# One fp32 encoder layer on one core: norm rows copied to SBUF, a finale of its own for the last token block, high parts first in gate and up, another pace for the norms

## The chip, the cores and the metric

The kernel runs on 1 core of one Trainium2 chip. The core has five engines with one in-order instruction queue each: TensorE (PE in the profile: matmuls and transposes), VectorE (DVE), ScalarE (ACT), GpSimd (POOL), and SyncE (SP), which here only issues DMAs. Operands stand in SBUF (128 partitions), matmul results in PSUM. The metric is the device time of one execution in microseconds.

## What is computed

One inference step of one encoder layer over 1024 prompt frames and 32 sample frames, D_MODEL 1024, in fp32: three sub-layers with a norm before and a norm after each, and a shift, scale and gate (adaLN) from a conditioning vector.

```python
# x += 1/2 * gate1 * RMSNorm_post(SwiGLU_1(adaLN(RMSNorm_pre(x))))
# x +=       gate2 * RMSNorm_post(W_out [GN_a(mixerA) ; GN_b(mixerB)](adaLN(RMSNorm_pre(x))))
# x += 1/2 * gate3 * RMSNorm_post(SwiGLU_2(adaLN(RMSNorm_pre(x))))
def rmsnorm(x, g):
    y = x * lax.rsqrt(jnp.mean(x * x, axis=-1, keepdims=True) + EPS)
    return y * g
def adaln_in(x, g, shift, scale):
    return rmsnorm(x, g) * (1 + scale[:, None, :]) + shift[:, None, :]
def swiglu(h, w_gate, w_up, w_down):
    return (jax.nn.silu(h @ w_gate) * (h @ w_up)) @ w_down
```

D_FF is 2816, that is 22 blocks of 128. The two mixers are banded attentions (8 heads with a cache of 512 rows; 8 query heads over 2 key heads with sinks); the change does not touch them. The outputs are y for prompt and sample, and the new cache rows.

## The kernel before

**Tiling.** Features stand on the partitions, tokens on the free axis, in three token blocks: tb0 and tb1 of 384 tokens, tb2 of 288 (256 of the prompt, 32 of the sample). A product in fp32 is made of three matmuls (`mm3`): weight and input are each split into a high and a low part, and hi·hi, hi·lo and lo·hi are added in PSUM. A weight block is split when it is loaded: ACT copies the high part (L303), DVE subtracts it for the low one (L304).

**Stages.** ffn1, attention (72 tiles), W_out (`out_piece`), ffn2, finale. A feed-forward stage runs through pairs of 128-wide blocks of D_FF. For each block and token block it makes `gate` (24 matmuls) and `up` (24) in one PSUM bank each, then ACT makes Silu of gate (`sl`, L550), DVE multiplies it by up (L551), ACT and DVE split the product into `gg` (L553, L554), and four `dn` groups of 12 matmuls are added to `facc` on DVE (L579 in the first round, L581 after). `gate` and `up` take turns in a pool of three PSUM banks (`p1`), so that the fourth of them waits until the first has been read.

**Norms.** `sumsq` squares a block on ACT (L364, tile `sq`, four pairs of feature tiles), folds and adds the pairs on POOL and DVE (L368, L370), and adds them over the partitions in two PE groups of three matmuls, `pss` (L357). `rstd_cols` makes the inverse root in ten tiny DVE operations in a row (rv at L387 to L391, ry, rt at L334 to L338). After WAIT = 3 more steps of the generator, three small matmuls spread it as a row over all partitions, `pr` (L405). `pss` and `pr` take turns in one PSUM bank (`pc`), and the readers of a row read `pr` there: eight scalings `n` of a pre-norm (L420), followed by h_hi on ACT (L444) and h_lo on DVE and POOL (L446, L449), or eight scalings of a post-norm's block (L464), followed by adding the residual (L467). The group norm of the mixers alone copies its row to SBUF first (L1145).

**What sets the order.** Norms and residuals are generators in a list (`side`); the feed-forward loops call `step(n)` after each gate and each up, which advances the list's first generator by n yields: PACE = 2, FAST = 10 in a stage's first round, OUTSTEP = 6 after each piece of W_out. That gives the order in which the program is written. A scheduler of the framework then sets the order on each engine, and takes an instruction forward where its inputs and its tile are free. Tiles come from pools that rotate; `s_tile` is a pool of five SBUF buffers, from which `sl` and the group norm's row are taken.

**Finale.** y = x + gate · norm(ffn2): for each token block the gates are multiplied onto f (L1304 on ACT, L1306 on DVE, eight of them), PE transposes f to tokens first (`py`, L1313, four to a bank), and DVE scales it by the token's inverse root and adds x, which was transposed before (`px`, L1293, copied to `xp` by ACT, L1294), at L1315. One DMA for each tile of 128 tokens writes y.

Of the kernel before, what the change touches and what calls it, by code (L numbers as in the profile page):

```python
# [34 lines left out]

PACE = 2
FAST = 10
OUTSTEP = 6
# [25 lines left out]
MANUAL = False  # L64
WAIT = 3
PREP = 3
STAGES = ((0, 34), (37, 54))
# [7 lines left out]
def encoder_step(ctx: ExitStack, tc, x_prompt, x_sample, cache_a_k, cache_a_v, cache_b_k, cache_b_v,  # L75
# [248 lines left out]
    def mm3(ps, w, k, hi, lo, start, stop):  # L324
        te.matmul(ps, w[:, 0, k], hi, start=start, stop=False)  # L325
        te.matmul(ps, w[:, 0, k], lo, start=False, stop=False)  # L326
        te.matmul(ps, w[:, 1, k], hi, start=False, stop=stop)  # L327


    def rsqrt(v, n, m):  # L330
# [13 lines left out]

    def sumsq(src, kts, w, bank, ends, fold=True):


        n = len(kts) // 2
        pss = bank("pss")
        cols = token_cols(w)  # L350
        behind = []

        def add_up(sq, first, last):
            halves = (0,) if fold else (0, 1)
            for q in halves:
                for j, (c0, m) in enumerate(cols):
                    te.matmul(pss[:m, j:j + 1], sq[:, q, c0:c0 + m], ones, start=first and j == 0 and q == 0,  # L357
                              stop=last and q == halves[-1], skip_group_check=True)

        acc, first = None, True  # L360
        for c in range(n):
            k = kts[2 * c]
            sq = h_tile([128, 2, 384], "sq")
            ae.activation(sq[:, :, :w], src[:, k:k + 2, :w], AF.Square)  # L364
            if fold:
                e = SQE[c % len(SQE)]
# [11 lines left out]
        add_up(*behind.pop())  # L378
        return pss

# [14 lines left out]

    def mean_rstd(src, kts, w, scale, ends, bank=None):

        bank = bank or pc
        pss = yield from sumsq(src, kts, w, bank, ends)
        y = rstd_cols(pss, w, scale)  # L400
        for _ in range(waits[0]):
            yield
        pr = bank("pr")
        for j, (c0, m) in enumerate(token_cols(w)):
            te.matmul(pr[:, c0:c0 + m], y[:m, j:j + 1].to_broadcast([m, 128]), ident[:m, :m], start=True, stop=True)  # L405
        yield
        return pr

    def norm_h(x, tb, j, H, ahead=0):
        w = TB[tb][1]  # L410
        r = yield from mean_rstd(x, range(KT), w, 1.0 / D, JN)
        hi, lo = H[tb] = (u_tile(tb, "h_hi", F32R), u_tile(tb, "h_lo", F32R))
# [41 lines left out]
    def resid(f, tb, j):  # L454

        w = TB[tb][1]
        r = yield from mean_rstd(f, range(KT), w, 1.0 / D, JR)
        for c in range(KT // 2):
# [66 lines left out]
    def ffn(key, H, F, wg, wu, wd, per_group, key_out, after, beside=lambda ff, tb: None):  # L525
# [10 lines left out]
        for r, (gi, blocks) in enumerate(plan):  # L536
# [3 lines left out]
            def up(ff, tb):  # L540
# [19 lines left out]
            def down(tb, r=r, grp=grp, wds=wds, gs=gs):  # L560
# [9 lines left out]
                for mp in range(KT // 2):  # L570
# [11 lines left out]
                    if r == final[tb]:  # L582
                        next(own)
                    step(1)
                if r == final[tb]:
# [18 lines left out]
            if (gi, 2) == (gi, blocks[-1]):  # L604
                per_group(gi)
        late.pop()()

# [530 lines left out]
    def group_norm(tb, g):  # L1138
# [3 lines left out]
        hi, lo = OH[tb]  # L1142
        pr = yield from mean_rstd(O[tb], range(4 * g, 4 * g + 4), w, 2.0 / D, JG, p1)
        r = s_tile([128, 384], "rstd")
        ae.activation(r[:, :w], pr[:, :w], AF.Copy)  # L1145
        for c in range(2):
# [134 lines left out]

    def tokens_first(tb):

        xp = upool.tile([128, 3, KT, 128], F32, name="xp", tag="u", bufs=6)
        for i, (t, c0, n) in enumerate(token_tiles(tb)):
            xt = XP[tb, i] = xp[:, i]
            xr = rpool.tile([128, KT, 128], F32, name="raw", tag="r")
            dma.dma_start(xr[:, :, :n], xs_dram[2][tb][:, :, c0:c0 + n])
            yield
            for hf in range(2):  # L1290
# [4 lines left out]
                yield  # L1295

    def finale(tb):
        f, w = F3[tb], TB[tb][1]
        pss = yield from sumsq(f, range(KT), w, pc, JF, fold=FF)
        y = rstd_cols(pss, w, 1.0 / D)  # L1300
        for k in range(KT):
            for a, b, st in SEGS[tb]:
                if k % 2:
                    ae.activation(f[:, k, a:b], f[:, k, a:b], AF.Copy, scale=gcoef[:, 2, st, k:k + 1])  # L1304
                else:
                    ve.tensor_scalar(f[:, k, a:b], f[:, k, a:b], gcoef[:, 2, st, k:k + 1], None, op0=OP.mult)  # L1306
            yield
        for i, (t, c0, n) in enumerate(token_tiles(tb)):
            xt = XP[tb, i]
            for k0 in (0, 4):  # L1310
                pt = p1("py", (128, 4, 128))
                for k in range(4):
                    te.transpose(pt[:n, k, :], f[:, k0 + k, c0:c0 + n], ident)  # L1313
                o = xt[:n, k0:k0 + 4]
                ve.scalar_tensor_tensor(o, pt[:n], y[:n, i:i + 1], o, op0=OP.mult, op1=OP.add)  # L1315
                yield
            dst = y_sample[0] if t == SEQ else y_prompt[0, t:t + 128]
            dma.dma_start(dst.rearrange("t (k c) -> t k c", c=128), xt[:n])
            yield

    def beside(ff, tb):
        if ff == NF - 1 and tb < 2:
            for t in ((0, 1), (2,))[tb]:
                begin(("xp", t), tokens_first(t))

# [30 lines left out]
```

## Time and profile before

| what | value |
| --- | --- |
| median of 3 runs | 2212.97 us (2211.99 to 2215.68) |
| the profiled execution | 2217.6 us, of which its span 2215.8 us |
| mean granted TensorE clock in it | 0.984 |
| PE busy | 2161.6 us (98%), 14012 instructions |
| DVE busy | 1239.1 us (56%) |
| ACT busy | 697.8 us (31%) |
| POOL busy | 179.2 us (8%) |

The span runs from the first instruction to the last. PE is busy nearly all the time, and all other engines far less, so PE's pauses, the clock it was granted and the work it was given are what the time is made of.

### The profile page before, as it was taken

The page shows a single profiled execution, that of the slowest core. Times are in us where ns is not written, and L with a number is a line of the kernel's source. Part 1 is how long each engine was busy: PE and PEld are TensorE (multiplying, and loading weights), DVE is VectorE, ACT ScalarE, POOL GpSimd, SP SyncE. Part 2 cuts the span into 40 slices and gives each one's busy share as a digit, 9 for nine tenths or more (in the row PEclk, how much of TensorE's full clock was granted, in tenths as well). Part 3 has the DMA queues.
Part 4 walks back from the last instruction along what each step waited for, and adds up shares of the span by engine and source line. Part 5 has one row for each costly group of instructions (what it writes and reads, how often), then busy time and mean ns, then how long its engine had stood idle before and what let it go on. Part 6 is the DMA issues. An engine that isn't in the chain of part 4 may idle for free.

```text
span 2215.8 us, 33976 instructions
## 1 busy us (share of the span) xinstructions
PE 2161.6 (98%) x14012; PEld 2068.6 (93%) x14012; DVE 1239.1 (56%) x2425; ACT 697.8 (31%) x1450; POOL 179.2 (8%) x281
## 2 busy tenths in 40 slices
PE   6999999999999999899999899999999999999998
PEld 4999999999999999799787589999999999999998
DVE  5788667874333497677444865785333333333336
ACT  4411111111121253576444663542111111111133
POOL 1100000000000023001110313220000000000000
PEclk8999999999999999899999899999999999999999
DMA  9253334434122352111112121424211111111122
GB/s 323 93 153 118 111 96 124 143 101 129 39 66 69 101 184 93 38 39 30 50 30 62 46 77 67 134 86 120 66 58 39 57 39 39 58 38 58 39 69 79
DMA packets 200623, 186.03 MB, mean 84 GB/s; under 512 B 7597, under 2 KB 169813, under 8 KB 199317
## 3 DMA queue, kind: packets, MB, share of 16 engines
q1 hardware_dynamic: 200468, 183.87, 27.1%
q8 instruction: 110, 1.80, 0.3%
q14 instruction: 45, 0.36, 0.1%
HBM read 164.12 MB, written 22.86 MB: 84 GB/s over the span
## 4 chain that ended last, share of the span: by engine, by line
PE 90%; DVE 4%; DMA 3%; ACT 1%; issue 1%; POOL 0%; SPq 0%; ACTq 0%; DVEq 0%; POOLq 0%
PE dn L325 7%; PE dn L326 7%; PE dn L327 7%; PE gate L327 7%; PE gate L326 7%; PE up L327 7%; PE up L326 7%; PE gate L325 7%; PE up L325 7%; PE po L713 3%; PE S L752 2%; PE pq L325 2%; PE pq L327 2%; PE pq L326 2%; DMA raw<-in_w_gate_dram 1%; PE pp L776 1%
## 5 line engine op out<-in xcount | busy, mean ns | idle before, releaser
L326 PE MATMUL gate<-h_lo,w 128*128 128x384 f32 (+1 forms) x1056 | 340.2, 322 | 4.0 <-DVE h_lo L446 4.0
L325 PE MATMUL dn<-gg,w 128*128 128x384 f32 (+1 forms) x1056 | 341.4, 325 | 1.1 <-DVE facc L581 1.0
L581 DVE TENSOR_TENSOR facc<-dn,facc 128x768 f32<-128x768 f32 (+1 forms) x240 | 212.9, 889 | 230.2 <-PE dn L327 229.9
L326 PE MATMUL dn<-gg,w 128*128 128x384 f32 (+1 forms) x1056 | 340.6, 323 | 0.6 <-DVE gg L554 0.6
L325 PE MATMUL gate<-h_hi,w 128*128 128x384 f32 (+1 forms) x1056 | 341.0, 323 | 0.0
L327 PE MATMUL gate<-h_hi,w 128*128 128x384 f32 (+1 forms) x1056 | 340.4, 322 | 0.0
L325 PE MATMUL up<-h_hi,w 128*128 128x384 f32 (+1 forms) x1056 | 340.2, 322 | 0.0
L326 PE MATMUL up<-h_lo,w 128*128 128x384 f32 (+1 forms) x1056 | 340.0, 322 | 0.0
L327 PE MATMUL dn<-gg,w 128*128 128x384 f32 (+1 forms) x1056 | 340.0, 322 | 0.0
L327 PE MATMUL up<-h_hi,w 128*128 128x384 f32 (+1 forms) x1056 | 339.9, 322 | 0.0
L304 DVE TENSOR_TENSOR w<-raw,w 128x1024 fp32r<-128x1024 f32 x187 | 231.5, 1246 | 150.5 <-ACT w L303 150.3
L303 ACT ACTIVATE w<-raw 128x1024 fp32r<-128x1024 f32 x187 | 195.7, 1056 | 266.1 <-PE dn L327 103.5
L550 ACT ACTIVATE sl<-gate 128x384 f32<-128x384 f32 (+1 forms) x132 | 60.9, 462 | 563.9 <-PE gate L327 560.9
L551 DVE TENSOR_TENSOR sl<-sl,up 128x384 f32<-128x384 f32 (+1 forms) x132 | 68.5, 519 | 292.1 <-PE up L327 286.1
L326 PEld LDWEIGHTS gate<-h_lo,w 128*128 128x128 f32 x1056 | 198.6, 188 | 4.6 <-DVE h_lo L446 4.6
L325 PEld LDWEIGHTS dn<-gg,w 128*128 128x128 f32 x1056 | 199.2, 189 | 1.6 <-DVE facc L581 1.2
L326 PEld LDWEIGHTS dn<-gg,w 128*128 128x128 f32 x1056 | 199.2, 189 | 1.0 <-DVE gg L554 0.9
L327 PEld LDWEIGHTS dn<-gg,w 128*128 128x128 f32 x1056 | 199.1, 189 | 0.0
L325 PEld LDWEIGHTS gate<-h_hi,w 128*128 128x128 f32 x1056 | 198.7, 188 | 0.1
L327 PEld LDWEIGHTS gate<-h_hi,w 128*128 128x128 f32 x1056 | 198.7, 188 | 0.0
L327 PEld LDWEIGHTS up<-h_hi,w 128*128 128x128 f32 x1056 | 198.7, 188 | 0.0
L325 PEld LDWEIGHTS up<-h_hi,w 128*128 128x128 f32 x1056 | 198.5, 188 | 0.0
(224 smaller groups left out, 3367.4 us busy)
## 6 DMA issues: line engine op xcount, KB each, us to landing
raw<-in_w_mod_dram SPq DMA_DIRECT2D x56, 512.0 KB, 4.0
raw<-in_w_gate_dram SPq DMA_DIRECT2D x54, 512.0 KB, 4.0
raw<-in_w_up_dram SPq DMA_DIRECT2D x54, 512.0 KB, 4.7
raw<-in_w_down_dram SPq DMA_DIRECT2D x54, 512.0 KB, 4.5
raw<-in_w_in_dram SPq DMA_DIRECT2D x18, 512.0 KB, 4.3
wm<-in_w_mod_dram SPq DMA_DIRECT2D x8, 1024.0 KB, 7.4
raw<-in_w_out_dram SPq DMA_DIRECT2D x13, 512.0 KB, 4.5
xr<-xs SPq DMA_DIRECT2D x16, 384.0 KB, 3.5
```

The costliest lines, as they stand in the source:

```text
L303: ae.activation(w[:, 0], r, AF.Copy)
L304: ve.tensor_sub(w[:, 1], r, w[:, 0])
L325: te.matmul(ps, w[:, 0, k], hi, start=start, stop=False)
L326: te.matmul(ps, w[:, 0, k], lo, start=False, stop=False)
L327: te.matmul(ps, w[:, 1, k], hi, start=False, stop=stop)
L550: ae.activation(sl[:, :w], ps[0][:, :w], AF.Silu)
L551: ve.tensor_tensor(sl[:, :w], sl[:, :w], ps[1][:, :w], op=OP.mult)
L581: ve.tensor_tensor(o, ps[:, :, :w], o, op=OP.add)
L713: te.matmul(po[64 * h:64 * h + 64, :n], vsl(j, h, kn), PT(h, j, kn), start=j == 0, stop=j == nt - 1)
L752: te.matmul(S[:, c:ce], self.T[:, h, :], KQ[:, 0, 128 * k0 + c:128 * k0 + ce], start=True, stop=True)
L776: te.transpose(pp[:, j - j0, :], P[:, 128 * j:128 * j + 128], ident)
```

## The change

1. `mm_all` takes the place of the loop over `mm3` in gate and up: for all eight feature tiles first hi·hi and lo·hi, which read h_hi alone, then the eight hi·lo, which read h_lo.
2. `mean_rstd` copies the row `pr` by ACT to an SBUF tile `rstd` of the `s_tile` pool (L423 in the changed kernel), for all norms but the very first, so that the bank `pc` is free after the copy.
3. `apart`: for tb2's norms (but the first), both its residuals, one group norm and the finale, the last pair of square tiles is not folded; PE adds its two halves itself, in three `pss` groups instead of two (three instead of one in the group norm).
4. `OUTWAIT = 4` in the loop over W_out's pieces: four steps instead of three between sums and row.
5. `step(BEHIND)` with BEHIND = 5 instead of PACE in rounds that run over tb2 alone.
6. The finale: POOL makes 16 diagonal matrices of the gates (`dg`), and PE multiplies f with them, which turns and scales f at once, in place of a transpose (and of the eight gate operations of each block). The finales of tb0 and tb1 are drained ahead of the last `dn` of tb2. tb2 has its own finale: x is turned behind the last `dn`, the four full half tiles wait in two `p2` banks, the sample's tile goes over ACT and POOL, and six half-tile DMAs write it.

```diff
+    def mm_all(ps, w, hi, lo):
+        for k in range(KT):
+            te.matmul(ps, w[:, 0, k], hi[:, k, :], start=k == 0, stop=False)
+            te.matmul(ps, w[:, 1, k], hi[:, k, :], start=False, stop=False)
+        for k in range(KT):
+            te.matmul(ps, w[:, 0, k], lo[:, k, :], start=False, stop=k == KT - 1)
...
-            halves = (0,) if fold else (0, 1)
+            halves = (0,) if fold and not (apart and last) else (0, 1)
...
-    def mean_rstd(src, kts, w, scale, ends, bank=None):
+    def mean_rstd(src, kts, w, scale, ends, bank=None, apart=False, copied=True):
         bank = bank or pc
-        pss = yield from sumsq(src, kts, w, bank, ends)
+        if apart:
+            ends = (len(kts) // 2 - 2, len(kts) // 2 - 1)
+        pss = yield from sumsq(src, kts, w, bank, ends, apart=apart)
         y = rstd_cols(pss, w, scale)
+        del pss
         for _ in range(waits[0]):
             yield
         pr = bank("pr")
...
+        if copied:
+            r = s_tile([128, 384], "rstd")
+            ae.activation(r[:, :w], pr[:, :w], AF.Copy)
+            pr = r
         yield
         return pr
...
                 for s in range(2):
-                    for k in range(KT):
-                        mm3(ps[s][:, :w], wgu[ff][s], k, hi[:, k, :], lo[:, k, :], k == 0, k == KT - 1)
-                    step(FAST if gi == 0 else PACE)
+                    mm_all(ps[s][:, :w], wgu[ff][s], hi, lo)
+                    step(FAST if gi == 0 else BEHIND if blocks == (2,) else PACE)
                 sl = s_tile([128, 384], "sl")
                 ae.activation(sl[:, :w], ps[0][:, :w], AF.Silu)
...
+        if key_out == "y":
+            finish()
         late.pop()()
...
+    waits[0] = OUTWAIT
     while outs:
         out_piece()
         step(OUTSTEP)
+    waits[0] = WAIT
...
+                ge.tensor_scalar(DG[st][:, k, :], ident, gcoef[:, 2, st, k:k + 1], None, op0=OP.mult)
...
+    def turned(pt, f, k, c0, n, t):
+        te.matmul(pt, f[:, k, c0:c0 + n], DG[1 if t == SEQ else 0][:, k, :], start=True, stop=True)
...
-        for k in range(KT):
-            for a, b, st in SEGS[tb]:
-                if k % 2:
-                    ae.activation(f[:, k, a:b], f[:, k, a:b], AF.Copy, scale=gcoef[:, 2, st, k:k + 1])
-                else:
-                    ve.tensor_scalar(f[:, k, a:b], f[:, k, a:b], gcoef[:, 2, st, k:k + 1], None, op0=OP.mult)
-            yield
+        if last:
+            yield from last_finale(f, y)
+            return
...
-                    te.transpose(pt[:n, k, :], f[:, k0 + k, c0:c0 + n], ident)
+                    turned(pt[:n, k, :], f, k0 + k, c0, n, t)
```

**Where instructions stand now.** In the rows below the number in a name grows in the order in which the program is written; a row stands for one or several instructions of its engine, in their order.

*The start of ffn2, PE.* Before, tb1's second norm has its sums (`pss_13745`) in the middle of the stage's fourth product, and its row `pr_13806` 16 matmuls later, among the `dn` groups:

```order
L327 MATMUL dn_14298<-gg_14143,w_13994 128x384
L325 MATMUL dn_14284<-gg_14280,w_13999 128x384
L325 MATMUL dn_14298<-gg_14280,w_13999 128x384
L405 MATMUL pr_13806<-ident_96,ry_13794 128x128 x3
L326 MATMUL dn_14284<-gg_14280,w_13999 128x384
```

In the changed kernel the same norm (`pss_13811`, `pr_13862`) and tb2's residual (`pss_14073`) stand in one piece behind the third product, gate of the second block:

```order
L335 MATMUL gate_14181<-h_hi_13566,w_14016 128x384
L337 MATMUL gate_14181<-h_lo_13567,w_14016 128x384 x8
L369 MATMUL pss_13811<-ones_98,sq_13804 128x1 x3
L369 MATMUL pss_13811<-ones_98,sq_13815 128x1 x3
L420 MATMUL pr_13862<-ident_96,ry_13824 128x128 x3
L369 MATMUL pss_14073<-ones_98,sq_14067 128x1 x2
L369 MATMUL pss_14073<-ones_98,sq_14067 32x1
L369 MATMUL pss_14073<-ones_98,sq_14071 128x1 x2
```

Behind the rest of `pss_14073` follow its row `pr_14099` and then the fourth product, `up_14182`: no matmul of the feed-forward stands any more between these two norms' sums and rows.

*The start of ffn2, ACT.* Before, the stage's first Silu (`sl_14140`, of the first product `gate_14002`), with the load of its table, stands behind the last weight split and ahead of the squares of tb1's second norm, though it was written behind them:

```order
L1177 ACTIVATE fo_13667<-wo_13946 128x288
L303 ACTIVATE w_14516<-raw_14514 128x1024
L550 ACT_TABLE_LOAD
L550 ACTIVATE sl_14140<-gate_14002 128x384
L364 ACTIVATE sq_13746<-fo_13251 128x768
```

Now the same Silu (`sl_14175`, of `gate_14034`) stands behind the copy of tb2's residual row, `rstd_14103`, which takes a tile of the same pool and is written ahead of it:

```order
L376 ACTIVATE sq_14067<-fo_13695 128x2x288
L376 ACTIVATE sq_14071<-fo_13695 128x2x288
L423 ACTIVATE rstd_14103<-pr_14099 128x288
L568 ACT_TABLE_LOAD
L568 ACTIVATE sl_14175<-gate_14034 128x384
L571 ACTIVATE gg_14178<-sl_14175 128x384
```

Ahead of these rows on ACT stand, all new ahead of the Silu, tb1's residual row, the squares and the row of tb1's norm and its h_hi.

*The end of ffn1, PE.* The norm of tb0 ahead of attention: before, 62 matmuls of gate, up and dn lay between its last sums (`pss_6661`) and its row `pr_6696`, which stands inside a gate:

```order
L325 MATMUL gate_7060<-h_hi_623,w_6904 128x288
L326 MATMUL gate_7060<-h_lo_624,w_6904 128x288
L327 MATMUL gate_7060<-h_hi_623,w_6904 128x288
L405 MATMUL pr_6696<-ident_96,ry_6684 128x128 x3
L325 MATMUL gate_7060<-h_hi_623,w_6904 128x288
```

Now the row follows its sums (`pss_6671`) at once, and an up follows the row:

```order
L328 MATMUL dn_6796<-gg_6566,w_6180 128x384
L329 MATMUL dn_6796<-gg_6566,w_6180 128x384
L369 MATMUL pss_6671<-ones_98,sq_6675 128x1 x3
L420 MATMUL pr_6696<-ident_96,ry_6684 128x128 x3
L334 MATMUL up_6815<-h_hi_627,w_6586 128x288
```

The residual of tb1 (`pss_6792`, `pr_6857`), and in the first round of ffn1 the norm of tb2 (`pss_594`, `pr_621`), stand in the same way.

*The end of ffn1, ACT.* Before, the Silus of these rounds stood among weight splits, with no norm's row between (`gate_6593` is the product whose bank the up behind next takes):

```order
L550 ACTIVATE sl_6557<-gate_6477 128x384
L303 ACTIVATE w_6585<-raw_6583 128x1024
L303 ACTIVATE w_6590<-raw_6588 128x1024
L553 ACTIVATE gg_6560<-sl_6557 128x384
L550 ACTIVATE sl_6653<-gate_6593 128x288
```

The same product is `gate_6599` now, its bank goes to `up_6815`, and its Silu stands right behind the copy of that norm's row:

```order
L305 ACTIVATE w_6934<-raw_6932 128x1024
L305 ACTIVATE w_6939<-raw_6937 128x1024
L423 ACTIVATE rstd_6700<-pr_6696 128x384
L568 ACTIVATE sl_6702<-gate_6599 128x288
L376 ACTIVATE sq_6754<-facc_887 128x768
```

On DVE the low parts of `w_6934` and `w_6939` stand between the sums and the inverse root of this norm; before, two such splits stood there too.

More of the change, by code (lines that the diff above doesn't have):

```diff
@@ L36 @@
 PACE = 2
+BEHIND = 5
 FAST = 10
@@ L65 @@
 WAIT = 3
+OUTWAIT = 4
 PREP = 3
@@ L410, in norm_h @@
         w = TB[tb][1]
-        r = yield from mean_rstd(x, range(KT), w, 1.0 / D, JN)
+        r = yield from mean_rstd(x, range(KT), w, 1.0 / D, JN, apart=tb == 2 and j > 0, copied=tb > 0 or j > 0)
         hi, lo = H[tb] = (u_tile(tb, "h_hi", F32R), u_tile(tb, "h_lo", F32R))
@@ L1142, in group_norm @@
         hi, lo = OH[tb]
[L1143 to L1145 removed]
+        r = yield from mean_rstd(O[tb], range(4 * g, 4 * g + 4), w, 2.0 / D, JG, p1, apart=(tb, g) == (2, 0))
         for c in range(2):
```

83 lines of the change are left out of this document (67 added, 16 removed).

## The prediction, made before the changed kernel was timed

> **What bounds the kernel now.** I read the page's busy times first, then the chain that ended last, the clock and busy time by stretch, and PE's waits.
>
> ```profile
> PE 2161.6 (98%) x14012; PEld 2068.6 (93%) x14012; DVE 1239.1 (56%) x2425; ACT 697.8 (31%) x1450; POOL 179.2 (8%) x281
> PE 90%; DVE 4%; DMA 3%; ACT 1%; issue 1%; POOL 0%; SPq 0%; ACTq 0%; DVEq 0%; POOLq 0%
> ```
>
> PE is busy for 2161.6 of 2215.8 us and makes 90% of the chain. So a change can take away PE's pauses (54 us in all), the slow clock behind them, and PE work; and whatever holds PE up anew costs its full length. The stretches that the change touches, as columns: window, its length, busy us of PE, PEld, DVE, ACT, POOL (instructions), granted clock, DMA share, GB/s.
>
> ```profile
> 60.00:80.00 20.00, 18.16 (x100) 17.76 (x99) 17.48 (x35) 11.73 (x20) 4.61 (x5) 0.91 0.56 172
> 760.00:780.00 20.00, 20.00 (x141) 20.00 (x140) 15.94 (x31) 6.67 (x10) 3.66 (x2) 1.00 0.49 143
> 780.00:800.00 20.00, 20.00 (x148) 19.92 (x146) 17.85 (x29) 10.38 (x14) 5.66 (x4) 1.00 0.66 211
> 880.00:900.00 20.00, 14.53 (x98) 13.45 (x97) 15.07 (x50) 11.46 (x32) 5.81 (x10) 0.74 0.14 59
> 1320.00:1340.00 20.00, 17.05 (x113) 15.01 (x112) 8.47 (x30) 8.21 (x16) 2.86 (x4) 0.86 0.36 105
> 1340.00:1360.00 20.00, 19.78 (x113) 19.27 (x113) 13.33 (x25) 9.18 (x15) 11.23 (x8) 0.97 0.00 1
> 1420.00:1440.00 20.00, 19.38 (x110) 19.20 (x109) 15.54 (x34) 6.78 (x12) 7.64 (x6) 0.91 0.27 105
> 1440.00:1460.00 20.00, 17.87 (x98) 17.49 (x97) 15.82 (x31) 7.65 (x13) 3.80 (x4) 0.91 0.23 60
> ```
>
> Read them in pairs of idle time and clock. 760 to 800, the end of ffn1 where tb0's and tb1's norms run, has no pause at all: nothing can be won there, only lost. 60 to 80 (first round of ffn1) has 1.84 us of pause and a clock of 0.91, which is 1.8 us of clock missing, or 3.6 us at half speed: **one pause of about 2 us also costs about 1.8 us of half clock**. 880 to 900 (tb2's norm ahead of attention), 1320 to 1360 (group norm of tb2) and 1420 to 1460 (start of ffn2) show the same. Whom PE waited for there:
>
> ```profile
> PE pr L405 <- DVE ry L338: 4.8, 2, 2.4
> PE gate L326 <- DVE h_lo L446: 4.0, 2, 2.1
> PE pk L1057 <- DVE n L420: 1.9, 1, 1.9
> ```
>
> **Prices.** One place of before shows what a row costs that follows its sums with no matmul between (tb2's norm; timeline: start, length, engine, what, idle before):
>
> ```profile
> 884.89 0.91 PE L357 MATMUL pss<-ones,sq 128*32 128x1 f32 x8
> 885.83 0.16 DVE L388 TENSOR_SCALAR rv<-pss 128x2 f32<-128x2 f32 x1 [1.19 <-PE pss L357]
> ...
> 887.93 0.16 DVE L338 SCALAR_TENSOR_TENSOR ry<-rt,ry 128x3 f32<-128x3 f32 x1
> 888.24 0.98 PE L405 MATMUL pr<-ident,ry 128*128 128x128 f32 x3 [2.44 <-DVE ry L338]
> ```
>
> The **row wait** is 2.44 us. The other durations, from the groups of 700 to 900 us and the timeline at the start of ffn2:
>
> ```profile
> L446 DVE SCALAR_TENSOR_TENSOR h_lo<-n,modT,h_hi 128x384 fp32r<-128x384 f32 x12 | 9.4, 838 | 0.0
> L467 DVE TENSOR_TENSOR facc<-facc,xr 128x768 f32<-128x768 f32 x4 | 4.4, 1132 | 0.0
> L550 ACT ACTIVATE sl<-gate 128x384 f32<-128x384 f32 x5 | 2.4, 488 | 17.1 <-PE gate L327 17.1
> ...
> 1415.56 0.34 PE L327 MATMUL gate<-h_hi,w 128*128 128x384 f32 x1
> 1415.74 0.83 PE L405 MATMUL pr<-ident,ry 128*128 128x128 f32 x6
> 1417.86 1.28 ACT L550 ACT_TABLE_LOAD   x1
> 1417.88 1.23 DVE L304 TENSOR_TENSOR w<-raw,w 128x1024 fp32r<-128x1024 f32 x1 [4.09 <-ACT w L303]
> 1419.02 4.28 DVE L464 SCALAR_TENSOR_TENSOR fo<-fo,gcoef,pr 128x384 f32<-128x384 f32 x8
> 1431.55 0.80 PE L357 MATMUL pss<-ones,sq 128*128 128x1 f32 x6 [0.62 <-DVE sq L370]
> ```
>
> A 384-wide matmul starts 0.18 us after the one before (1415.56 to 1415.74), so gate or up of 24 takes 4.2; the 288-wide ones 3.2 in proportion. A row's copy is not in the trace: another 128x384 read of PSUM by ACT, Silu, takes 0.49, and I take that (nothing if it were hidden, 0.6 at most). In the changed order a Silu stands right behind the copy of a row, and the next up needs that Silu's bank. So each such row has a **hold**: copy 0.49, Silu 0.49, two hand-overs, 1.1 us (1.0 for 288). A `pss` group is 0.7 (0.91 for eight records, of which a group has six).
>
> **The change, stage by stage.**
>
> *First round of ffn1.* High parts first and the copied rows remove the pause on h_lo and its half clock: −3.6. New: tb1's row is followed by the hold (1.1), tb2's sums come 0.6 late, its row follows at once (2.44), then another hold (1.0): 5.1, and half clock behind two of these pauses (2 × 1.8): +8.7. Net **+5.1** (+2 to +8).
>
> *End of ffn1, tb0 and tb1.* Nothing is removed. Along the four norms: (1) tb0's residual: 3.1 us of matmuls cover the row wait; hold 1.1; then `dn` waits for gg's low part, which DVE makes behind two scalings, two adds of 1.1 and a weight split, 1.8. (2) tb0's norm: row wait 2.44 and two weight splits of 1.23 inside the chain, 4.9; hold 1.0. (3) tb1's residual: its sums stand on DVE behind eight scalings (4.3), six h_lo (5.0 at 838 ns), Silu's products, a split and folds, about 13 us from the row, while PE has gate, up and four `dn`, 7.2, behind the hold: 4.7; then 0.4 of a split, 2.44 and a hold of 1.0; the next gate waits for a bank whose reader stands behind eight scalings, 1.0. (4) tb1's norm: 12 `dn` (1.6) lie between sums and row, but the chain of 2.44 has an addition to facc and two splits inside, 5.6: 4.0; hold 1.0. Together 23.3. PE bounds only some of the work between, so I put half clock behind three pauses, 5.4: **+28.7** (+13, bare row waits and holds, to +37).
>
> *tb2's norms ahead of attention.* BEHIND ends the other chains early; 5 to 6 us of other products now lie between tb2's sums and both rows, and the bank is free for `pk`. The stretch 880 to 900 loses 5.5 us of pause, and 0.26 × 20 = 5.2 us of missing clock, of which some 3.3 fall on work: −8.8; two more `pss` groups: +1.4. **−7.4** (−8.8 to −4).
>
> *Group norm of tb2.* 19 matmuls of W_out (0.18 each at 384, 3.4) cover the row wait of 2.44. Gone are 3.2 us of pause (2.95 and 0.22) and 3.4 of missing clock, less what falls on the pauses: −6.1, plus two groups 1.4: **−4.7** (−6 to −2). OUTWAIT moves rows only among W_out's matmuls, which keep PE busy: nothing; if that cover were gone, a row wait.
>
> *Start of ffn2.* Count from the end of tb1's residual row. PE has 21 matmuls of up and 24 of gate: 8.0 us, then only sums and rows until the Silu. DVE and ACT: copy 0.5; from the first scaling (1419.02) to the second sums (1431.55) before took 12.5, less 0.5 for one product that now comes later: sums at 12.5, row wait from 13.2, row done at 16.5. Copy 0.5, scalings 4.3, six h_lo 4.7 (between 0.7 and 0.84), folds 1.0: tb2's sums start at 27.0 and take 2.1, row wait, row: 32.4. Copy, table 1.28, Silu: the fourth product starts at 34.7. Of the 26.7 us since 8.0 PE works 5.0: 21.7 of pause. Behind it tb2's norm: row wait 2.44, hold 1.0, a bank 1.8. Half clock behind three pauses 5.4. Sum +32.3. Gone are 2.75 us of pause and 0.18 × 20 = 3.6 of half clock: **+26** (+14 to +34).
>
> *Finale.* Rows of the chain:
>
> ```profile
> 2189.73 0.44 PE py L1313 x4
> 2198.49 0.67 DVE facc L581
> 2206.39 0.18 DVE ry L334
> 2208.36 0.76 DVE xp L1315
> 2212.09 0.74 DVE xp L1315
> ```
>
> A transpose is 0.11; an fp32 product with a diagonal is not shown, but three such products of `pr` take 0.83, 0.28 each, and two records of transposes 0.22, which I take (0.11 to 0.28). The 48 of tb0 and tb1 come ahead of the last `dn`: 2.6 more for tb0, 5.3 for tb1, 2.6 less for tb2's turned x: last `dn` +5.3. Behind it 16.9 us remain before (2198.9 to 2215.8); now sums after about 5.3, root 2.3, four scalings 2.7, and 3.0 to the end as before: 13.3. **+1.7** (−3 to +5).
>
> Sum: 5.1 + 28.7 − 7.4 − 4.7 + 26 + 1.7 = 49.4. The profiled execution took 2217.6, so 2267; the median of the three runs is 4.6 lower: **2262**.
>
> **Rivals.**
>
> *Bare waits.* DVE and ACT are ahead more than I count, and only row waits (seven of 2.44, one of them half covered) and holds remain, without half clock: low ends, 2 + 13 − 8.8 − 6 + 14 + 0 = +14, **2227**. For it speaks the engine's share of 56%; against it, 760 to 800 shows DVE busy 16 to 18 of 20.
>
> *No clock loss.* If pauses of 1 to 3 us leave the clock alone, the 14.4 us of half clock fall out: **2248**. The row 60 to 80 speaks against it. [...]
>
> *Rows from SBUF are slow to read.* The group norm's scalings, which read a copied row, against those that read PSUM (1300 to 1400 us):
>
> ```profile
> L1150 DVE SCALAR_TENSOR_TENSOR z<-o,cst,rstd 128x384 f32<-128x384 f32 x4 | 3.4, 900 | 0.0
> L420 DVE SCALAR_TENSOR_TENSOR n<-fo,acoef,pr 128x384 f32<-128x384 f32 x8 | 4.3, 608 | 0.0
> ```
>
> 0.29 more for each of eight scalings in five chains that PE now waits for is +11.7: **2274**. [...]
>
> *The other side: not slower.* Removed are 3.6 + 8.8 + 6.1 + 6.3 = 24.8 us. If every new pause is bare and short, ffn2's Silu comes after tb1's row instead of tb2's in effect (sums ready when PE arrives), then seven row waits and eight holds are 24.5, less 4 that pieces of `dn` cover: −4, **2209**. It decides once the start of ffn2 pauses for less than about 8 us. The order of ACT, in which that Silu stands behind tb2's copied row, speaks against it.
>
> **How the numbers follow.** My forecast 45%, bare waits 19%, no clock loss 14%, slow rows 13%, not slower 9%. The range takes in the forecast's neighbours, half of the bare case and the slow rows: 2229 to 2284. A measurement tells about 0.2% (4.4 us) from no change. Faster 4%, same 5%, slower 91%.
>
> **What would show it.** Right: PE's waits list `pr` behind DVE's ry with some 15 to 20 us in seven or more pauses, up behind ACT's Silu with 10 or more; 740 to 800 no longer full; a pause of 15 us or more in pieces behind the third product of ffn2, and none at 880 to 900 and 1330. Wrong: PE still full over 740 to 800, or the first Silu of ffn2 starting within 10 us of its gate; then the Silus do not wait for the rows.

## The result, and the profile after

| | before | changed kernel |
|---|---|---|
| median, us (4 runs each) | 2213.64 | 2295.53 |
| lowest to highest, us | 2211.99 to 2215.68 | 2294.24 to 2295.83 |
| profiled execution, us (its span) | 2217.6 (2215.8) | 2294.24 (2292.4) |

The changed kernel is slower: the ratio is 1.0369, with a 95% interval of 1.0353 to 1.0386. That is 82 us, where 49 were forecast, and the time lies above the range.

The page of the changed kernel, busy times of the engines and the chain that ended last:

```profile
PE 2185.3 (95%) x14132; PEld 2095.1 (91%) x14132; DVE 1238.4 (54%) x2401; ACT 696.6 (30%) x1450; POOL 192.9 (8%) x297
PE 34%; DVE 1%; ACT 0%; issue 0%; POOLq 0%; POOL 0%; ACTq 0%; DVEq 0%
```

PE is busy 24 us longer, but the span grew by 76.6: PE's pauses went from 54 to 107 us. DVE's total is as before (1238.4 against 1239.1): the changed finale takes some 13 us off it (1225.9 in e7 below) and slower scalings put 14 back (1224.0 in e3, without them). What the pauses come from is shown by the experiments.

Busy time by stretch of the changed kernel; columns as in the prediction (window, length, busy us of PE, PEld, DVE, ACT and POOL, granted clock, DMA share, GB/s):

```profile
780.00:800.00 20.00, 15.22 (x99) 14.57 (x99) 18.29 (x20) 6.04 (x8) 8.32 (x5) 1.00 0.46 158
800.00:820.00 20.00, 12.62 (x71) 12.03 (x69) 17.34 (x31) 12.82 (x21) 6.16 (x5) 0.74 0.20 55
820.00:840.00 20.00, 13.28 (x69) 12.64 (x70) 15.63 (x29) 4.23 (x7) 6.28 (x4) 0.66 0.48 160
1460.00:1480.00 20.00, 10.68 (x55) 10.01 (x53) 13.94 (x27) 4.52 (x7) 7.84 (x6) 0.72 0.19 80
1480.00:1500.00 20.00, 5.20 (x24) 4.74 (x24) 13.54 (x32) 8.58 (x16) 5.20 (x5) 0.50 0.20 59
```

The end of ffn1, which was full, and the start of ffn2 now have long pauses, and the granted clock is low behind them, down to 0.50 where PE is busy for 5.2 of 20 us. Whom PE waited for, over the whole span (us in total, times, longest):

```profile
PE pr L420 <- DVE ry L348: 20.5, 7, 4.6
PE pss L369 <- POOL sq L382: 16.4, 4, 5.9
PE pss L369 <- DVE sq L382: 14.2, 2, 12.3
...
PE up L334 <- ACT sl L568: 8.6, 8, 2.3
PE gate L334 <- DVE sl L569: 3.2, 2, 1.7
```

Rows wait for the inverse root in seven places, sums wait for the squares, and up waits for the Silu eight times. Gate waits for what the Silu is multiplied into. Before, the first kind was 4.8 in two places, and no matmul waited for a Silu.

The table cuts the span at the same matmuls of both traces and gives what each stretch takes longer than before, in us. The first round of ffn1 and the start of ffn2 run from the first to about the 200th gate of their stage, the end of ffn1 from the 1441st gate to the first product of attention. The last columns are experiments told of below.

| stretch | forecast | changed | e1 | e2 | e3 | e4 | e11 |
|---|---|---|---|---|---|---|---|
| first round of ffn1 | +5.1 | +10.2 | +9.7 | +0.6 | −1.3 | +11.9 | +0.5 |
| end of ffn1 | +28.7 | +37.7 | +22.0 | −0.2 | +0.3 | +22.0 | −0.3 |
| tb2's norms ahead of attention | −7.4 | −7.9 | −2.1 | +12.4 | +4.9 | −1.0 | +1.6 |
| attention, to its last product | | −5.3 | −5.2 | −6.4 | −5.2 | −4.3 | −3.2 |
| W_out, group norm of tb2 | −4.7 | +4.7 | +0.5 | +3.8 | +4.6 | +4.0 | −0.8 |
| start of ffn2 | +26 | +33.1 | +30.8 | +0.7 | −3.9 | +32.5 | −4.1 |
| finale (to last dn, and behind it) | +1.7 | +4.8 | 0 | +4.4 | +4.6 | +4.1 | −0.6 |

Attention is shorter in every kernel, even where nothing near it was touched. In the profiled execution of before, the time from the first `S` product to the first product of W_out is 213.7 us at a mean granted clock of 0.95; it is 209.5 at 0.98 in the changed kernel and 209.1 at 0.98 in e7, which changes nothing there. So this row is in the main the clock of that one execution, which fits its lying above its median. How far two executions differ elsewhere shows in e3 and e6, which have the same lines in both feed-forward stages: their first rounds of ffn1 differ by 2.4 us and their starts of ffn2 by 2.5. A single step of that size says little.

### The profile page after: what moved, and what is told of

It reads as the page before. It is cut to its first block, busy times and chain, and to the rows that moved or that the text cites. A ratio compares the mean times of both kernels' runs of the same rounds, so it can differ in the third digit from the quotient of the medians.

```text
span 2292.4 us, 34227 instructions
## 1 busy us (share of the span) xinstructions
PE 2185.3 (95%) x14132; PEld 2095.1 (91%) x14132; DVE 1238.4 (54%) x2401; ACT 696.6 (30%) x1450; POOL 192.9 (8%) x297
## 5 line engine op out<-in xcount | busy, mean ns | idle before, releaser
L334 PE MATMUL gate<-h_hi,w 128*128 128x384 f32 (+1 forms) x1056 | 332.1, 323 | 4.4 <-DVE sl L569 3.2
L335 PE MATMUL gate<-h_hi,w 128*128 128x384 f32 (+1 forms) x1056 | 330.1, 322 | 0.0
L334 PEld LDWEIGHTS up<-h_hi,w 128*128 128x128 f32 x1056 | 204.4, 194 | 10.3 <-ACT sl L568 10.3
L335 PEld LDWEIGHTS up<-h_hi,w 128*128 128x128 f32 x1056 | 204.5, 194 | 0.0
L337 PE MATMUL gate<-h_lo,w 128*128 128x384 f32 (+1 forms) x1056 | 196.2, 322 | 0.6 <-DVE h_lo L465 0.6
L337 PE MATMUL up<-h_lo,w 128*128 128x384 f32 (+1 forms) x1056 | 193.0, 324 | 0.0
L337 PEld LDWEIGHTS up<-h_lo,w 128*128 128x128 f32 x1056 | 174.6, 191 | 0.0
```

Of the source, the lines that this page charges most:

```text
L334: te.matmul(ps, w[:, 0, k], hi[:, k, :], start=k == 0, stop=False)
L335: te.matmul(ps, w[:, 1, k], hi[:, k, :], start=False, stop=False)
L337: te.matmul(ps, w[:, 0, k], lo[:, k, :], start=False, stop=k == KT - 1)
```

## The experiments

Each kernel was measured beside the kernel before on the same chip, so its ratio counts more than its microseconds. Where an expectation names theories by letters: A is that the copied rows take tiles from the pool of the Silus (`s_tile`, five tiles, handed out in program order), so that a Silu, and PE behind it, stands behind a norm's row; C is that other parts of the change cost the time; H, that half clock does; G, that the chain of the group norm has a length of its own; S, that scalings which read a row from SBUF are slow beside POOL.

**e1: of the whole change, the copies alone.**

```diff
         pr = bank("pr")
...
+        if copied:
+            r = s_tile([128, 384], "rstd")
+            ae.activation(r[:, :w], pr[:, :w], AF.Copy)
+            pr = r
```

> The kernel before, with part 2 alone: every row but the first is copied into a tile of the pool from which Silu's tiles come. Theory A (the Silus stand behind the rows, because a pool hands out its tiles in the order in which the program asks for them, so PE has no free bank and waits for rows): nearly all of the loss is there, 2265 to 2292 us, with the steps of the first round of ffn1 (about +10) and of the start of ffn2 (about +33) as in the changed kernel, and a smaller one at the end of ffn1 (+15 to +35), since PACE 2 leaves matmuls between two of its norms' sums and rows. Rival C (the faster pace of rounds over tb2 alone, high parts first or the extra sums bring the pauses): 2210 to 2235 us.

Measured: 2273.56 us, ratio 1.0258 (1.0240 to 1.0275). These lines make 57 of the 82 us, at the three places where the changed kernel loses most. C falls as the main cause; what `BEHIND` adds is in e4.

**e2: the whole change, with the copies in tiles of another pool.**

```diff
-            r = s_tile([128, 384], "rstd")
+            r = h_tile([128, 384], "rstd")
```

> The changed kernel, rows copied all the same, but into tiles of the pool that holds the squares (one word changed). Theory A: the Silus stand ahead of the rows again, 2195 to 2215 us, and PE's waits list no up behind ACT's Silu. Rival B (the copy on ACT and the scalings that read SBUF are themselves the cost, about 0.5 us and 8 times 0.3 us at each of 20 rows on the path): still above 2270 us.

Measured: 2231.89 us, ratio 1.0070 (1.0055 to 1.0085). One word is worth 3.0%, some 66 us, with the same instructions, in another order. ACT's timeline at the start of ffn2 in this kernel (start, length, engine, line, what, idle before):

```profile
1426.06 1.28 ACT L568 ACT_TABLE_LOAD   x1
1428.87 0.49 ACT L568 ACTIVATE sl<-gate 128x384 f32<-128x384 f32 x1 [1.52 <-PE gate L337]
1430.11 0.49 ACT L423 ACTIVATE rstd<-pr 128x384 f32<-128x384 f32 x1 [0.75 <-PE pr L420]
```

The Silu waits only for its own gate, and stands ahead of the residual row; PE's waits list no up behind a Silu any more. In the changed kernel it stands behind that row and two more:

```profile
1458.54 0.49 ACT L423 ACTIVATE rstd<-pr 128x384 f32<-128x384 f32 x1 [4.01 <-PE pr L420]
...
1478.41 0.49 ACT L423 ACTIVATE rstd<-pr 128x384 f32<-128x384 f32 x1 [7.85 <-PE pr L420]
...
1498.26 0.41 ACT L423 ACTIVATE rstd<-pr 128x288 f32<-128x288 f32 x1 [9.82 <-PE pr L420]
1498.69 1.28 ACT L568 ACT_TABLE_LOAD   x1
1499.98 0.49 ACT L568 ACTIVATE sl<-gate 128x384 f32<-128x384 f32 x1
```

Its gate was done at 1457; the Silu runs at 1500. The mechanism is shown: with the pool, the order on ACT changes and the loss goes. But the level was expected at 2195 to 2215: tb2's norms ahead of attention lose 12.4 here where the changed kernel gains 7.9. In the changed kernel 5.5 us of other products lie between tb2's sums and its row; here PE waits 4.4 us for these sums, 2.4 for the row right behind them and 2.8 for an h_lo. `BEHIND` is in both kernels, so it brings that gain only together with the late end of ffn1, which costs more.

**e3: the whole change without the copies (only the group norm keeps its own).**

```diff
-        if copied:
+        if copied and bank is not pc:
```

> The changed kernel without part 2: rows stay in their bank, as before (the group norm keeps its copy). Theory A: 2195 to 2215 us, within 8 us of e2_rows_h; what separates the two is the price of the copies themselves. Rival B: 2195 to 2215 us too, but over 50 us under e2_rows_h. Rival C: above 2250 us.

Measured: 2226.71 us, ratio 1.0046 (1.0028 to 1.0063). The loss at the three places is gone. What remains are tb2's norms, the group norm and the finale, together some 14 us, and against them some 5 at the two places where high parts first was to gain. It was expected lower, as e2 was: the other parts of the change, taken together, do not pay either. Some 5 us lie between e2 and e3; so much do the copies cost when no Silu stands behind them.

**e4: the whole change without `BEHIND`.**

```diff
-                    step(FAST if gi == 0 else BEHIND if blocks == (2,) else PACE)
+                    step(FAST if gi == 0 else PACE)
```

> The changed kernel without part 5 (PACE 2 in the rounds over tb2 alone). Theory A: only the end of ffn1 changes, where two norms now have 5 us of matmuls between sums and row: its step falls from +38 to about +20, 2275 to 2283 us in all, while the first round of ffn1 and the start of ffn2 keep their +10 and +33. Rival C: the end of ffn1 loses its whole step, about 2258 us.

Measured: 2285.45 us, ratio 1.0310 (1.0294 to 1.0325). The steps are as expected; the time is 2 us above what was named, and the kernel before took 2216.89 beside it, 3 more than beside the changed kernel. With the copies in, `BEHIND` adds 15.7 us at the end of ffn1 (22.0 to 37.7) and takes 6.9 off tb2's norms; without the copies (e3) it costs nothing there.

**e5 and e9: the changed kernel with PE kept busy in its pauses.** Products of the identity with itself, which nobody reads, stand ahead of seven rows and three sums.

```diff
+                for _ in range(warm):
+                    te.matmul(banks[0][:, 128:256], ident, ident, start=True, stop=True)
...
+        for _ in range(warm[1]):
+            te.matmul(pr[:, 384:512], ident, ident, start=True, stop=True)
```

> The changed kernel with 133 more fp32 matmuls of the identity by itself, whose results nothing reads, put on PE ahead of seven rows and three sums, where PE pauses. Theory H (half clock: the pauses themselves set the clock down, and the matmuls behind them then run at half speed, some 20 us of the loss beyond the pauses): PE's pauses in these three stages shrink by 20 us or more, the clock is above 0.9 at the end of ffn1 and at the start of ffn2, and the time falls by 8 to 18 us although PE does more: 2278 to 2288. Rival (the slow matmuls behind the pauses have another cause, say SBUF or PSUM traffic of the norms): the time stays or grows, 2294 to 2310.

Measured: e5 2293.09 us, ratio 1.0344 (1.0328 to 1.0360), between what the two theories named. Its trace has 284 records more on PE, two for each of 142 products (66 ahead of sums, 76 ahead of rows; not 133). Two of its stretches, to be held against those of the changed kernel above:

```profile
800.00:820.00 20.00, 13.63 (x101) 12.78 (x101) 18.02 (x31) 11.17 (x19) 6.05 (x5) 0.88 0.26 73
1480.00:1500.00 20.00, 15.85 (x113) 15.22 (x111) 12.73 (x31) 7.76 (x14) 4.49 (x5) 0.83 0.20 59
```

The clock rose from 0.74 to 0.88 and from 0.50 to 0.83 (theory H had it above 0.9), yet the end of ffn1 took 37.2 us more than before (37.7 without the fill) and the start of ffn2 31.9 (33.1). Only the first round of ffn1 was shorter by more, +6.4 instead of +10.2. DVE's busy time in these rows is about the same. But at the start of ffn2, 9 products ahead of a row ran for 3.4 and 4.2 us where PE had waited 2.3, so they could have hidden a gain. Hence a second dose, with about half as many ahead of the rows (5 ahead of most) and the same number ahead of the sums, 109 in all.

> e5_warm with fewer idle products ahead of the rows (5 in place of 9, so that they end within the 2.3 us for which PE waits there; in e5_warm they ran 3.4 us and delayed the rows). Theory H (half clock on the sums, the rows and what follows them costs some 10 us): a ratio to the kernel before of 1.026 to 1.031, where the changed kernel has 1.037. Rival: 1.033 to 1.038, for the stretches are as long as their chain on DVE and ACT, and a faster PE in them helps little.

Measured: 2291.63 us, ratio 1.0346 (1.0332 to 1.0360); the three stretches took +7.7, +38.7 and +31.7. H falls but for a few us: the two long stretches keep their length though PE is kept busy, which says that they are as long as the chains of DVE and ACT through them. The rows' own products still ran slowly at the start of ffn2 (0.42 us each in e5, 0.43 in e9, 0.29 before), so the price of the clock is bounded here, not measured.

**e6: e3, and the group norm's sums as before.**

```diff
-        r = yield from mean_rstd(O[tb], range(4 * g, 4 * g + 4), w, 2.0 / D, JG, p1, apart=(tb, g) == (2, 0))
+        r = yield from mean_rstd(O[tb], range(4 * g, 4 * g + 4), w, 2.0 / D, JG, p1, apart=False)
```

> e3_no_copy with the folded sums of before in tb2's group norm. Theory G (the chain from these sums over row, scalings, o_lo and squares to the next group norm's sums takes 14.5 us whatever PE does, and 48 matmuls of W_out lie in it before and after; covering the row's wait only moved the pause to the next sums): the stage keeps a pause of 5 to 6 us, and only the two more sums (1.4) and their place go, so the step of W_out falls from +4.6 to +1 to +3.5, in all 2222 to 2226. Rival (the third step OUTWAIT or the unfolded sums caused the pause): the step falls to 0 or under, the pause to under 3 us.

Measured: 2226.72 us, ratio 1.0042 (1.0029 to 1.0054). The stretch of W_out goes from +4.6 to +3.3; a pause of 5.93 us ahead of the second group's sums stays. PE's timeline of the changed kernel around it:

```profile
1366.17 0.65 PE L369 MATMUL pss<-ones,sq 128*128 128x1 f32 x6
...
1367.74 1.34 PE L369 MATMUL pss<-ones,sq 128*128 128x1 f32 x12
...
1372.41 0.94 PE L420 MATMUL pr<-ident,ry 128*128 128x128 f32 x6
...
1383.64 1.20 PE L369 MATMUL pss<-ones,sq 128*128 128x1 f32 x6 [5.93 <-POOL sq L382]
```

And of the kernel before:

```profile
1332.89 0.76 PE L357 MATMUL pss<-ones,sq 128*128 128x1 f32 x6 [0.58 <-POOL sq L370]
1336.01 1.76 PE L405 MATMUL pr<-ident,ry 128*128 128x128 f32 x6 [2.36 <-DVE ry L338]
1348.12 0.76 PE L357 MATMUL pss<-ones,sq 128*128 128x1 f32 x6 [0.22 <-POOL sq L370]
```

From the end of the sums to the next group's sums it is 14.5 us in both (1333.65 to 1348.12, 1369.08 to 1383.64). But that these are equal is chance: it is 15.5 in e6 and 13.7 in e11. What is fixed is the way from the end of the row to the next sums: 10.3 us in all four (10.35, 10.29, 10.30, 10.36), through the scalings, o_lo and the squares on DVE, ACT and POOL. Before, PE has all 48 matmuls of W_out that lie between the two sums behind the row, and they fill these 10.3 us. With `OUTWAIT` = 4, 24 of them stand ahead of the row (in the changed kernel 5 of these between the sums); the row comes 4.2 us behind the sums in e6 where it waited 2.4, and only 24 matmuls are left behind it. So the wait for the row goes, and one of 5.93 comes at the next sums. The pauses at these sums and this row are 6.5 us in e6 and 3.2 before, which is the +3.3. No run changes `OUTWAIT` alone, but e2, e3, e4 and e6, with four steps, have a pause of 5.2 to 5.9 there, and e1, e7, e8 and e11, with three, one of 0.3 at most. So theory G was right that covering the row's wait moves the pause, and its rival was right that the third step makes it.

**e7: before, with the finale alone.**

```diff
+    def last_finale(f, y):
...
-                    te.transpose(pt[:n, k, :], f[:, k0 + k, c0:c0 + n], ident)
+                    turned(pt[:n, k, :], f, k0 + k, c0, n, t)
```

> The kernel before with part 6 alone (and the finale's three sum groups). Theory F (the diagonal products ahead of the last dn cost 6 us, the shorter tail gives 1.4 back): 3 to 6 us above the kernel before, all of it behind the start of ffn2. Rival (what is left of the loss in e3_no_copy comes from the attention stages alone): within 2 us of the kernel before.

Measured: 2219.19 us, ratio 1.0009 (1.0001 to 1.0018). In its trace, counted from the 200th gate of ffn2, the last `dn` comes 6.3 us later and the end behind it takes 1.4 less, which makes 4.9, as theory F had it; by the ratio the whole is only some 2 (0.2 to 4), so the times alone do not tell F from its rival. Either way the finale does not pay.

**e8: a selection.** High parts first, `BEHIND`, and only tb2's residual and norm ahead of attention copied and summed apart; the finale and the group norm are those of before.

```diff
-        if copied:
+        if bank is not pc or which:
...
-        r = yield from mean_rstd(x, range(KT), w, 1.0 / D, JN, apart=tb == 2 and j > 0, copied=tb > 0 or j > 0)
+        r = yield from mean_rstd(x, range(KT), w, 1.0 / D, JN, apart=tb == 2 and j == 1, which=tb == 2 and j == 1)
```

> High parts first in gate and up, BEHIND, and for tb2's two norms ahead of attention alone copied rows and unfolded sums; finale, group norm and OUTWAIT as before. From the steps measured so far: first round of ffn1 -1.3, start of ffn2 -4 to -5, the norms ahead of attention -2 (the bank is free earlier, but the row still follows its sums): 2204 to 2211 us, faster than both kernels. Rival (high parts first gives nothing once the order of all engines is new): 2212 to 2220.

Measured: 2214.33 us, ratio 0.9992 (0.9982 to 1.0001): not told from before, and above what was expected. The first round of ffn1 (−2.9) and the start of ffn2 (−5.5) gain what was named, but tb2's norms took +6.5 where −2 was expected.

**e10: the changed kernel, with POOL's share of the residual adds given to DVE.**

```diff
+POOL_ADDS = ()
```

> The changed kernel with all residual adds on DVE, none on POOL. Theory S (a scaling that reads its row from SBUF has two SBUF inputs and is slowed by POOL's adds beside it, not by SBUF as such): the post-norms' scalings fall from 1.0 to about 0.6 us a piece, 8 in 4.3 us instead of 7.5, while DVE has two more adds of 1 us at each of five residuals; in all within 8 us of the changed kernel. Rival (rows in SBUF are slow to read by themselves): they stay at 0.9 to 1.0 us.

Measured: 2299.30 us, ratio 1.0382 (1.0366 to 1.0397). The groups of DVE's scalings by a row, columns: busy us, mean ns of one, idle before. First the changed kernel:

```profile
L483 DVE SCALAR_TENSOR_TENSOR fo<-fo,gcoef,rstd 128x384 f32<-128x384 f32 x16 | 15.0, 1008 | 8.5 <-ACT rstd L423 8.5
...
L439 DVE SCALAR_TENSOR_TENSOR n<-fo,acoef,rstd 128x384 f32<-128x384 f32 x16 | 9.9, 690 | 3.0 <-ACT rstd L423 3.0
```

Then e3, where they read the row from PSUM, and e10:

```profile
L483 DVE SCALAR_TENSOR_TENSOR fo<-fo,gcoef,pr 128x384 f32<-128x384 f32 x16 | 8.6, 610 | 4.7 <-PE pr L420 4.7
```

```profile
L483 DVE SCALAR_TENSOR_TENSOR fo<-fo,gcoef,rstd 128x384 f32<-128x384 f32 x16 | 8.7, 614 | 8.5 <-ACT rstd L423 8.5
```

S is shown for the post-norms' scalings: 1008 ns with the row in SBUF and POOL adding beside them, 614 with the row in SBUF and no adds on POOL, 610 with the row in PSUM and the adds on POOL (e3). So neither SBUF nor POOL alone made them slow; how the two together do it no run shows. The mean of 1008 hides two kinds: in the changed kernel's trace twelve of the sixteen take 0.61 us and four 2.2. Each of the four starts inside one of POOL's adds and ends 0.4 us behind it; the first add behind tb1's row is this one, and the scaling beside it runs from 1461.72 to 1463.93:

```profile
1461.35 2.16 POOL L486 TENSOR_TENSOR fo<-fo,xr 128x768 f32<-128x768 f32 x1 [13.81 <-DVE fo L483]
```

The pre-norms' scalings stayed at 689 in e10, against 610 in e3: two of those sixteen are slow (1.4 and 1.1 us), each beside a fold of squares on POOL (L380), which e10 leaves there. The kernel gained nothing, since DVE now had the adds themselves: the end of ffn1 went from +37.7 to +45.4, the start of ffn2 only from +33.1 to +30.3.

**e11: before, with high parts first alone.**

```diff
-                    for k in range(KT):
-                        mm3(ps[s][:, :w], wgu[ff][s], k, hi[:, k, :], lo[:, k, :], k == 0, k == KT - 1)
+                    mm_all(ps[s][:, :w], wgu[ff][s], hi, lo)
```

> The kernel before with part 1 alone (high parts first). From the steps of e3_no_copy and e8_best2: first round of ffn1 -1 to -3, start of ffn2 -4 to -5.5, the rest as before: 2 to 8 us under the kernel before, ratio 0.996 to 0.999. Rival (these steps came from other parts): within 1.5 us, ratio 0.9993 to 1.0007.

Measured: 2212.32 us against 2216.95 of before beside it, ratio 0.9983 (0.9973 to 0.9993). It is the only version whose interval lies below the kernel before, by less than the 0.2% that the prediction took as the bound. The start of ffn2 gains 4.1, where the prediction put down 6.3. The first round of ffn1 gains nothing (+0.5, expected −1 to −3); PE's waits from 44 to 100 us in this kernel:

```profile
PE pt L624 <- ACT h_hi L448: 2.5, 1, 2.5
PE pt L624 <- ACT xt L626: 1.5, 1, 1.5
```

The wait of 1.8 for h_lo is gone, and one for the input's transposes stands in its place.

## Why the prediction was wrong, point by point

**Right** were the side, the mechanism and the places. The Silus stand behind the copied rows, PE runs dry between a norm's sums and its row, and the loss sits at the end of ffn1 and the start of ffn2; e2 shows that this is the change's whole loss but for some 15 us. Most signs named beforehand came: seven waits of `pr` for ry with 20.5 us (15 to 20 were named), 780 to 800 no longer full, and a wait of 12.3 in a stretch of 34 us (1466 to 1500) with nothing but sums and rows, behind the third product of ffn2. Up behind the Silu fell a little short (8.6 us; 10 or more were named), and a pause was to be gone at the group norm, where 5.9 stay. Taking 4.6 us off for the profiled execution was right too: the row of attention above has about that much (−5.3), and it is the clock of that execution.

**Wrong** were the sizes, nearly all to the same side, and one sign. The terms add to 49.4; the stretches that they stand for measured 82.6. The one step of reasoning that failed is "OUTWAIT moves rows only among W_out's matmuls, which keep PE busy: nothing", and the terms that were most too small are those of the end of ffn1 and the start of ffn2. Of the 33 between:

*Group norm of tb2 (−4.7; +4.7).* "19 matmuls of W_out cover the row wait" was true, and worth nothing: `OUTWAIT` took them from behind the same row, where they had filled the 10.3 us that DVE, ACT and POOL need from the row to the next sums. The pause moved there (5.93), which costs 3.3 in e6, and the two groups more of sums came on top (1.4; e6 takes off 1.3).

*tb2's norms ahead of attention (−7.4; −7.9).* The size came, but partly by luck. The reason given was that `BEHIND` ends the other chains early; in e2, with `BEHIND` and without the late Silus, the stretch loses 12.4, so the gain came only with the loss ahead of it, which the forecast did not link to it.

*End of ffn1 (+28.7; +37.7).* The pauses were right: 23.3 forecast, and 1.6 became 25.6. Slow matmuls (starts further apart than is usual for the same matmul) were put at 5.4 and grew by 11.7, and the rest, extra sums above all, by some 2. Yet in e5 and e9 the stretch stays as long (+37.2, +38.7) with more of the clock granted (a mean of 0.89 and 0.85 over 780 to 860, 0.81 in the changed kernel), which points to the chain through DVE and ACT as the term that was too small. The scalings of two residuals took 8 × 0.39 more each (994 ns in the groups of the changed kernel, 608 in e3) and those of two norms 8 × 0.10 (708 against 605), together some 8 us; how much of that PE saw was not separated, as e10 moved the adds onto DVE.

*Start of ffn2 (+26; +33.1).* Counted from the end of tb1's row, the fourth product was forecast at 34.7 and came at 42.0 (1458.50 to 1500.53), which is the whole miss. PE's timeline there:

```profile
1457.67 0.83 PE L420 MATMUL pr<-ident,ry 128*128 128x128 f32 x6
...
1471.72 2.72 PE L369 MATMUL pss<-ones,sq 128*128 128x1 f32 x12 [5.38 <-POOL sq L382]
1476.75 1.62 PE L420 MATMUL pr<-ident,ry 128*128 128x128 f32 x6 [2.31 <-DVE ry L348]
1490.67 3.44 PE L369 MATMUL pss<-ones,sq 128*128 128x1 f32 x18 [12.29 <-DVE sq L382]
1496.47 1.75 PE L420 MATMUL pr<-ident,ry 128*128 128x128 f32 x6 [2.36 <-DVE ry L348]
1500.53 0.69 PE L334 MATMUL up<-h_hi,w 128*128 128x384 f32 x1 [2.30 <-ACT sl L568]
```

Waits for ry and the last hold came as priced (2.3 to 2.4). What was missing stands in DVE's timeline of the changed kernel, and in the sums and rows above:

```profile
1459.07 7.50 DVE L483 SCALAR_TENSOR_TENSOR fo<-fo,gcoef,rstd 128x384 f32<-128x384 f32 x8 [3.28 <-ACT rstd L423]
...
1478.94 4.86 DVE L439 SCALAR_TENSOR_TENSOR n<-fo,acoef,rstd 128x384 f32<-128x384 f32 x8 [2.33 <-ACT rstd L423]
...
1483.72 5.28 DVE L465 SCALAR_TENSOR_TENSOR h_lo<-n,modT,h_hi 128x384 fp32r<-128x384 f32 x6
```

Against the forecast the first sums end 2.7 us later (15.9; 13.2), their row 3.4 (19.9; 16.5), tb2's sums start 5.2 later (32.2; 27.0) and its row ends 7.3 later (39.7; 32.4). On DVE the residual's eight scalings took 7.50 instead of 4.28, of which other work hides a part, the norm's eight 4.86 instead of 4.3 and six h_lo 5.28 instead of 4.7. On PE, at a granted clock of 0.50, the two rows took 1.62 and 1.75 instead of the 0.83 of the first row above, which had 1.00, and tb2's sums 3.44 instead of 2.1, some 3 us together.

*First round of ffn1 (+5.1; +10.2).* Rows and holds came as forecast (2.4 and 1.8). New and not foreseen are waits of the input's transposes:

```profile
PE pt L638 <- DMA X<-in_x_prompt_dram: 2.8, 1, 2.8
...
PE pt L638 <- ACT xt L640: 1.5, 1, 1.5
```

Before, PE waited 0.3 us there. The pre-norm's h_hi and h_lo, 1.9 us of wait (1.8 before), did not go either. e11 shows a wait for the input with part 1 alone, and gains nothing; e3 and e8 gain 1.3 and 2.9. So of the −3.6 credited to this order, no run shows the whole.

*Finale (+1.7; +4.8).* The last `dn` came 6.2 later, for 5.3. The end behind it was shortened by 1.4, not 3.6: it now hangs on the sample's tile, which goes through ACT and then POOL,

```profile
2288.21 1.25 POOL L1387 TENSOR_TENSOR xp<-yz,xp 32x512 f32<-32x512 f32 x1 [0.31 <-ACT yz L1386]
```

2 us behind the last of DVE's scalings (2287.47); its write ends the span.

**The rivals.** "Bare waits" and "not slower" fell with the pauses. "No clock loss" is half right by e5: the clock did fall (0.50 in 1480 to 1500), but it mattered little there, where PE waits for DVE anyway (with 0.83 in e5 the start of ffn2 still took +31.9 instead of +33.1). "Slow rows" was true in that the post-norms' scalings took 1008 ns with a copied row and 610 without, though only beside POOL's adds (614 in e10, without them), and it was made a rival of the forecast at 13% where it was a term that adds to it: 2262 and its 11.7 reach 2274, and the range ended 10 us above that. Its price came not as 0.29 on each scaling but as some 1.6 us for each scaling that meets an add on POOL (2.2 instead of 0.61), two to a post-norm of 384 tokens. The terms were summed from undisturbed durations, and nearly all misses had one sign (tb2's norms alone came out 0.5 lower), so a range made of the terms' single ends was too narrow.

**Open:** how the 9 us too few at the end of ffn1 divide between slow scalings and low clock; and why tb2's norms lose 5 to 12 us in e2, e3 and e8. Of that, e7 and e11, which change nothing there, also lose 2.3 and 1.6, and two more groups of sums are put at 1.4.

## What to carry to other kernels

A tile pool shared between two users orders them: before a new user takes tiles from a pool, look whose next request then stands behind it on its engine, and who waits for that one. Covering a wait with work that already filled the next wait of the same chain only moves the pause (here 2.36 us at the row went and 5.93 came at the next sums); measure the chain from the row to the next sums, and count the work on each side of the row. Where a forecast is a sum of chains that an idle PE waits for, prices from undisturbed stretches can be too low, as nearly all were here; a slowdown that the author knows of is then a term, not a rival.

## What the runs showed that was not expected

The post-norm's scaling on DVE cost the same with its row in SBUF as in PSUM (614 ns in e10 and 610 in e3, for 128x384) as long as POOL did not add beside the first; in the changed kernel the scalings that started inside an add lasted until 0.4 us behind the add's end, 2.2 us in all. And filling PE's pauses with idle products brought the granted clock back (0.50 to 0.83 in one stretch of e5), with about 1 us of gain in a stretch of 140 us (+31.9 instead of +33.1): the whole ratio is 1.0344 and 1.0346 against 1.0369, with intervals that overlap.
